# Two layers of attention, RWKV-7 and gated MLP on one core: a new order of emission in the mixings, and norm factors spread by VectorE

## The chip, the cores and the metric

The kernel runs on one core of one Trainium2 chip, in one launch. The metric is device time in microseconds (us), lower is better. Three runs of the kernel before took 2082.16, 2076.11 and 2067.94 us, median 2076.11 us.

## The reference, cut to what matters

There are 256 context tokens and 256 latent tokens of width 1024, and two layers. Each layer has a mixing part and a SwiGLU part. In the mixing part three branches read the same normalised input h: windowed attention, a bidirectional RWKV-7, and a spatial gating unit (SGU). They are merged by sigmoid gates and projected out. The RWKV branch sets the order of the work around the change:

```python
kk = heads((k * lp['k_k']).astype(f32))
kk = kk * lax.rsqrt(jnp.sum(kk * kk, -1, keepdims=True) + 1e-12)
...
S = S * w[..., None, :] + sa[..., :, None] * b[..., None, :] + v[..., :, None] * k[..., None, :]
...
mu = jnp.mean(y, -1, keepdims=True)
var = jnp.mean(jnp.square(y - mu), -1, keepdims=True)
y = ((y - mu) * lax.rsqrt(var + GN_EPS)).reshape(B, T, C) * lp['ln_w'] + lp['ln_b']
```

The state S passes through the context first and then through the latent tokens, in both directions. There are 8 heads of 64; the two `rsqrt` above give one factor for a head and a token.

## The kernel before, in words

Activations stand with channels on the 128 partitions and 512 tokens (context, then latent) in the free dimension. Dense products run as three fp32r products of split operands (high and low parts), so a weight tile of 128x1024 is loaded by SyncE's queue (`wtile`, L163), split by ScalarE (high part, L129) and VectorE (low part, L130), and used by 24 matmuls for one 128-row output (L92). Results go to two PSUM buffers with the tag `mm` that all dense products of the mixing share.

`phase_ab` (one call for each layer) holds the whole mixing up to the merge. It is written as Python generators, and each `yield` ends a stage:

- **K0 to K3** (`t_common`), one for a pair of heads: projections of k, r and v (stages 0 to 2; in layer 1 also the value residual in stage 2), norm of k (3 and 4), in-context rates (5), bonus (6). The norm is made by `rnorm` and `rnorm2`: squares are summed by TensorE (L423), the reciprocal root is computed by VectorE in some 12 small instructions (L136 to L142), GpSimd spreads it over 64 columns a head (the tile `rx`, L428), and TensorE transposes that (L436) for the multiplication.
- **P0 to P7** (`t_prep`), one for a unit, that is one pair of heads and one stream: unit 2h is pair h in the context, unit 2h+1 pair h in the latent tokens. Stage 0 makes the decay's matmuls (`pw`) and its tanh, stage 1 the cumulated decay (`pc`) and its exponentials, 2 the tile AR, 3 and 4 the tile BK with a scratch tile `gg` each, 5 to 8 four groups of score products (`psc`, L591, each taken from PSUM by VectorE into SC, L592), 9 to 11 transposes (`pvs`, `pbk`).
- **I0 to I7** (`t_inv`): a triangular inverse by VectorE, 31 steps of two dependent instructions (L645, L646), and small matmuls (`piy`, `pi`).
- **C0 to C7** (`t_chain`): four steps of the recurrence, each a few matmuls and short copies (`cw`, `cu`, `cn`, `py`); unit i waits for unit i-1.
- **Q0 to Q3** (`t_post`), a pair's end: group norm of y, also by `rnorm` and `rnorm2` (sums in `pm` and `gns`, scratch tiles `sqy` and `rx`), bonus, gate, and a store to DRAM by GpSimd's queue (L762).
- **G** (24 gate projections, tile `gps`, each stored by ScalarE's queue, L375), **A** (attention's q, k, v: matmuls `ptm`, transposes `pq`), **T** (attention: scores `sc`, transposes `pt`, output `po`), **S** (SGU), **X** (modulation vectors of layer 0, with weight loads on SyncE's queue).

The order is written out by hand. `slots` gives every stage a time from the numbers in `CB[layer]["SL"]`: pair h starts at `per`*h, K, P, C and Q are offsets, `P2` and `C2` shift the odd unit, the capital letters G, A, T, X, S start a series and the small letters are its steps. The stages are emitted by sorted time; `need` emits first what a stage depends on. The emitted program is then placed on the engines' queues, where a stage of a kind with a `PRI` of n is ranked as if it stood n instructions earlier; the dense matmuls of G and K keep their emitted order among themselves (`DENSE`). On chip each engine works through its queue in order.

Tiles with a tag share a few buffers: the tag `tmp` has 3 (`sgw`, `gg`, `sqk`, `sqy`, `rx`, `sm`, and in layer 1 `vf` and `sg`), the PSUM tags `rw` 1 (`pw`, `pc`, `psc`, `pvs`, `pbk`), `rc` 2 (`kns`, `knb`, `pa`, `pbn`, `pu`, `pm`, `gns`, `gnb`, `pg`, `pq`, `sc`, `pt`, `po`), `mm` 2. SC has 2 buffers, so unit i+2 can write its scores when unit i's chain has ended. The tile v has one buffer, so the next pair's v has to wait for the odd unit's `pvs`.

After `phase_ab` come `phase_m` (merge and output projection) and `phase_f` (SwiGLU), which the change does not touch.

Of the kernel before, what the change touches and what calls it, by code (L numbers as in the profile page):

```python
# [19 lines left out]
T = 256  # L20
# [7 lines left out]
DENSE = ("G", "K")  # L28
NX = 12
WR = 3  # L30
CB = [
    dict(SL={'per': 77.5, 'K': 10, 'P': 34.7, 'P2': 12, 'I': 108.0, 'C': 55.2, 'C2': 20, 'Q': 140, 'G': 120, 'g': 14, 'T': 120, 't': 4, 'A': 60, 'a': 5, 'S': 0, 's': 5.8, 'X': 60, 'x': 8},
         PRI={'C': 4000, 'I': 3000, 'P': 6000, 'K': 500, 'Q': 2000, 'T': 0, 'A': 0, 'S': 0, 'G': 0},
         PB={'rw': 1, 'rc': 2, 'ch': 1},
         GV=(1, 3),
         BF={'k': 2, 'v': 1, 'bv': 2, 'r': 1, 'kk': 2, 'th': 1, 'tmp': 3, 'ap': 2, 'aPT': 2, 'SC': 2, 'AR': 2, 'VS': 2, 'BKT': 2, 'BK': 1, 'ix': 1, 'gx': 1, 'gy': 1}),
    dict(SL={'per': 57.6, 'K': -18.7, 'P': 24.9, 'P2': 10.0, 'I': 95.9, 'C': 37.4, 'C2': 10.9, 'Q': 99.4, 'G': 62.8, 'g': 14.9, 'T': 73.7, 't': 6.1, 'A': 20, 'a': 4, 'S': -20, 's': 0.5, 'X': 32.2, 'x': 8},
         PRI={'C': 4000, 'I': 4000, 'P': 6000, 'K': 500, 'Q': 3000, 'T': 0, 'A': 0, 'S': 0, 'G': 0},
         PB={'rw': 1, 'rc': 2, 'ch': 1},
         GV=(1, 3),  # L40
         BF={'k': 2, 'v': 1, 'bv': 2, 'r': 1, 'kk': 2, 'th': 1, 'tmp': 3, 'ap': 2, 'aPT': 3, 'SC': 2, 'AR': 2, 'VS': 3, 'BKT': 2, 'BK': 1, 'ix': 2, 'gx': 1, 'gy': 1}),
]
DUR = dict(K=(5.5, 5.5, 5.5, 3, 1.5, 2, 5), P=(1.5, 2, 1, 3.5, 3.5, 1, 1, 1, 1, 1.5, 3, 1), I=(2.5,) * 9, C=(1.2,) * 12, Q=(2, 3, 1.5, 1), G=())


# [40 lines left out]
def trunk(ctx: ExitStack, tc: tile.TileContext, out, a):  # L86
# [11 lines left out]
    V = nc.vector  # L98
    S = nc.scalar
    G = nc.gpsimd  # L100
# [31 lines left out]
    def rsqrt(pool, out, x, scale, bias, tag):  # L132

        xs = pool.tile(list(out.shape), F32, tag=tag + "x", bufs=1, name="rsx")
        t = pool.tile(list(out.shape), F32, tag=tag + "t", bufs=1, name="rst")
        V.tensor_scalar(xs, x, scale * RS_A, bias * RS_A, op0=ALU.mult, op1=ALU.add)  # L136
        V.tensor_scalar(t.bitcast(I32), xs.bitcast(I32), 1, 0x7fffffff, op0=ALU.logical_shift_right, op1=ALU.bitwise_xor)
        V.tensor_scalar(out, t, RS_B, None, op0=ALU.mult)
        for _ in range(3):
            V.tensor_mul(t, out, out)  # L140
            V.scalar_tensor_tensor(t, t, -0.5 / RS_A, xs, op0=ALU.mult, op1=ALU.mult)
            V.scalar_tensor_tensor(out, t, 1.5, out, op0=ALU.add, op1=ALU.mult)  # L142
# [234 lines left out]
    def phase_ab(L, extra):  # L377

        l = L.l
        cb = CB[l]  # L380
        last = l == DEPTH - 1
# [3 lines left out]
        with tc.tile_pool(name="pb", bufs=1, reuse_waits="tile", side="right") as pb, tc.tile_pool(name="pe", bufs=1, reuse_waits="tile") as pe, tc.tile_pool(name="pbp", bufs=1, space=PSUM, reuse_waits="tile") as pbp:  # L385

            def rw(shape, name):
                return pbp.tile(shape, F32, tag="rw", bufs=cb["PB"]["rw"], name=name)

            def rc(shape, name):  # L390
                return pbp.tile(shape, F32, tag="rc", bufs=cb["PB"]["rc"], name=name) if "rc" in cb["PB"] else rw(shape, name)

            def tmp(name, n=512):
                return pe.tile([128, n], F32, tag="tmp", bufs=cb["BF"]["tmp"], name=name)

            def tmc(name, n=512):
                return pb.tile([128, n], F32, tag="tmc", bufs=cb["BF"]["tmc"], name=name) if "tmc" in cb["BF"] else tmp(name, n)

# [12 lines left out]
            def pj(f, s0, y):  # L411
                w = wtile(a["w_fm"][l, f])
                ps = pmm.tile([128, 512], F32, tag="mm", name="rps")
                n = 512 - 256 * s0
                proj(ps[:, :n], w, slice(256 * s0, 512), cl="K", l=l)
                conv(ps[:, :n], f, y, 2 - s0)

            def rnorm(sq, n, scale, bias, name):

                nt = n // 128  # L420
                pss = rc([128, 4, 2], name + "s")
                for j in range(nt):
                    mm(pss[:, j], sq[:, 128 * j:128 * j + 128], bones[:, 0:128:64], start=True, stop=True)  # L423
                rn = pb.tile([128, 4, 2], F32, tag="rn", bufs=2, name="rn")
                rsqrt(pb, rn[:, :nt], pss[:, :nt], scale, bias, "rr")
                rx = tmc("rx")
                rxv = rx[:, :n].rearrange("p (a h d) -> p a h d", h=2, d=64)
                G.tensor_tensor(rxv, rn[:, :nt].unsqueeze(3).broadcast_to([128, nt, 2, 64]),  # L428
                                ones[:, 0:64].unsqueeze(1).unsqueeze(1).broadcast_to([128, nt, 2, 64]), op=ALU.mult)
                return rx  # L430

# [16 lines left out]
            if last:  # L448

                vraw = tmc("vraw", KT * 32)  # L450
                nc.sync.dma_start(vraw, a["vrd"].rearrange("p k r -> p (k r)"))
                vhl = pe.tile([128, 512], F32R, tag="tmp", bufs=cb["BF"]["tmp"], name="vhl").rearrange("p (a b) -> p a b", a=2)
                vh, vl = vhl[:, 0], vhl[:, 1]
# [20 lines left out]
            def t_common(hp):  # L474

                h = H[hp]
                hc = slice(128 * hp, 128 * hp + 128)
                h.kT = kT = pe.tile([128, 512], F32, tag="k", bufs=cb["BF"]["k"], name="kT")
                pj(4 + hp, 0, kT)
                yield  # L480
                h.r = r = pe.tile([128, no], F32, tag="r", bufs=cb["BF"]["r"], name="r")
                pj(hp, so, r)
# [18 lines left out]
                sq = tmc("sqk")  # L501
                S.activation(sq, kT, AF.Square, scale=kkc)
                rx = rnorm(sq, 512, 1.0, 1e-12, "kn")
                yield
                rn = rnorm2(rx, 512, "kn")
# [173 lines left out]
            def t_chain(i):  # L679
# [8 lines left out]
                if emit:  # L688
                    py = pbp.tile([128, 8, 64], F32, tag="y", bufs=1, name="py")
                    mm(py.rearrange("p c j -> p (c j)"), zero, zero[:, 0:1].broadcast_to([1, 512]), start=True, stop=False)  # L690
                ch = lambda name: pbp.tile([128, 2, 64], F32, tag="ch", bufs=cb["PB"]["ch"], name=name)
                for c in range(4):
# [48 lines left out]
            def t_post(hp):  # L741

                need("C", 2 * hp + 1, 99)
                h = H[hp]
                y = h.y
                pm = rc([128, 512], "pm")
                mm(pm[:, :no], bones, y, start=True, stop=True)
                V.scalar_tensor_tensor(y, pm[:, :no], -1.0 / 64, y, op0=ALU.mult, op1=ALU.add)
                sq = tmc("sqy")
                S.activation(sq[:, :no], y, AF.Square)  # L750
                yield
                rx = rnorm(sq, no, 1.0 / 64, 64e-5, "gn")
                yield
                V.tensor_mul(y, y, rnorm2(rx, no, "gn"))
                V.tensor_scalar(y, y, pv[:, V_LW + hp:V_LW + hp + 1], pv[:, V_LB + hp:V_LB + hp + 1], op0=ALU.mult, op1=ALU.add)
                need("K", hp, 99)
                G.tensor_add(y, y, h.bv)
                yield
                pg = rc([128, 512], "pg")
                mm(pg[:, :no], L.gup[:, 128 * hp:128 * hp + 128], sxg, start=True, stop=True)  # L760
                V.tensor_mul(y, y, pg[:, :no])
                G.dma_start(orw_d[:, hp, 256 * so:512], y)  # L762
                yield
# [210 lines left out]
            def advance(kind, i):  # L974
# [3 lines left out]
                if done[key] == 99:  # L978
                    return
                with tc.high_priority(cb["PRI"].get(kind, 0)):  # L980
                    done[key] = 99 if next(live[key], live) is live else done[key] + 1
# [127 lines left out]
    with tc.tile_pool(name="px", bufs=1, side="right") as px, tc.tile_pool(name="pxp", bufs=1, space=PSUM) as pxp:  # L1109
        x = px.tile([128, KT, 512], F32, name="x0")  # L1110
# [17 lines left out]
    for l in range(DEPTH):  # L1128
# [8 lines left out]
        with tc.tile_pool(name="pw", bufs=1, reuse_waits="tile") as pw, tc.tile_pool(name="px", bufs=1, reuse_waits="tile", side="right") as px, tc.tile_pool(name="pxp", bufs=1, space=PSUM, reuse_waits="tile") as pxp:  # L1137
            x = px.tile([128, KT, 512], F32, name="x")
# [120 lines left out]
```

## Time and profile before

| what | value |
|---|---|
| median of three runs | 2076.11 us |
| the profiled execution's own time | 2055.66 us |
| its span, first to last instruction | 2053.9 us |
| TensorE (matmul) busy | 1913.0 us, 93% of the span |
| VectorE busy | 1355.0 us, 66% |
| ScalarE busy | 854.5 us, 42% |
| GpSimd busy | 237.7 us, 12% |
| mean granted TensorE clock | 0.943 |
| share of the last-ending chain: PE, DVE, DMA, ACT, issue, POOL | 74%, 12%, 4%, 4%, 4%, 1% |

The mixing of layer 0 lies between 48 us and 727 us of the span, that of layer 1 between 1245 us and 1775 us. PE is TensorE's matmuls, DVE VectorE, ACT ScalarE, POOL GpSimd. "Idle before" is the time in which an engine had nothing to run, and the name behind the arrow is what ended it.

### The profile page before, as it was taken

To read this page: it belongs to the slowest core of one execution; us is meant where nothing else is said; L and a number is where in the kernel's file an instruction comes from. 1 tells how busy PE (TensorE), PEld (TensorE's weight loads), DVE (VectorE), ACT (ScalarE), POOL (GpSimd) and SP (SyncE) were. 2 spreads that over 40 slices of the span, in tenths; PEclk is the share of its full clock that TensorE was granted. 3 is DMA by queue.
4 is the path that set the end of the run, shared out by engine and by line. 5 is a ranking of instruction groups with operands and counts; after the bars stand their busy time and mean duration, and the time that the engine had idled before them with its cause. 6 is when DMAs were issued, how large, how long until landed. Compare 5 with 4: busy or idle time off the path is not lost.

```text
span 2053.9 us, 35061 instructions
## 1 busy us (share of the span) xinstructions
PE 1913.0 (93%) x13162; PEld 1527.6 (74%) x13162; DVE 1355.0 (66%) x3657; ACT 854.5 (42%) x1848; POOL 237.7 (12%) x401
## 2 busy tenths in 40 slices
PE   4999989999999989899999997889998999698999
PEld 3877776666666768787887885777776777598999
DVE  4587776477585445688656545696786877476665
ACT  3442333444354433432232334444444555255443
POOL 3111201101001012100000002212020201120000
PEclk8997999989999999999999998988997999599999
DMA  8222213221211585166556422311220222374553
GB/s 286 78 67 79 63 47 114 83 90 53 63 39 55 202 269 163 62 188 212 176 175 212 145 79 76 100 66 32 93 69 14 74 75 88 122 230 146 185 183 105
DMA packets 97094, 239.16 MB, mean 116 GB/s; under 512 B 9594, under 2 KB 25082, under 8 KB 96796
## 3 DMA queue, kind: packets, MB, share of 16 engines
q1 hardware_dynamic: 88860, 223.82, 33.9%
q10 hardware_dynamic: 6912, 9.44, 1.3%
q0 software_dynamic: 1152, 3.67, 0.5%
q8 instruction: 103, 1.69, 0.3%
q14 instruction: 67, 0.55, 0.1%
HBM read 219.59 MB, written 17.30 MB: 115 GB/s over the span
## 4 chain that ended last, share of the span: by engine, by line
PE 74%; DVE 12%; DMA 4%; ACT 4%; issue 4%; POOL 1%; SPq 0%; ACTq 0%; POOLq 0%; DVEq 0%
PE fps L92 17%; PE gps L92 8%; PE rps L92 5%; PE psc L591 3%; PE yps L1094 3%; PE yps L1095 3%; PE yps L1096 3%; DVE wl L130 2%; PE sc L865 2%; DMA mr<-in_w_mod 2%; PE py L701 2%; PE po L893 2%; PE py L730 1%; PE cw L696 1%; PE ops L1026 1%
## 5 line engine op out<-in xcount | busy, mean ns | idle before, releaser
L129 ACT CAST wh<-wr 128x512 fp32r<-128x512 f32 (+1 forms) x560 | 341.7, 614 | 579.2 <-PE fps L92 196.8
L130 DVE TENSOR_TENSOR wl<-wr,wh 128x512 fp32r<-128x512 f32 (+1 forms) x560 | 389.6, 701 | 236.7 <-ACT wh L129 203.7
L92 PE MATMUL fps<-hh,wh 128*128 128x256 f32 (+1 forms) x720 | 241.3, 338 | 2.2 <-ACT hh L351 2.2
L92 PE MATMUL fps<-hh,wl 128*128 128x256 f32 (+1 forms) x720 | 241.6, 336 | 0.0
L92 PE MATMUL fps<-hl,wh 128*128 128x256 f32 (+1 forms) x720 | 240.9, 336 | 0.7 <-POOL hl L356 0.7
L92 PEld LDWEIGHTS fps<-hh,wh 128*128 128x128 f32 x720 | 138.3, 193 | 17.3 <-ACT hh L351 3.0
L92 PEld LDWEIGHTS fps<-hl,wh 128*128 128x128 f32 x720 | 138.3, 193 | 14.0 <-POOL hl L356 1.1
L92 PEld LDWEIGHTS fps<-hh,wl 128*128 128x128 f32 x720 | 138.7, 193 | 12.8
L92 PE MATMUL gps<-hh,wh 128*128 128x512 f32 (+1 forms) x384 | 142.1, 370 | 2.8 <-DVE itp L645 1.4
L92 PE MATMUL gps<-hl,wh 128*128 128x512 f32 (+1 forms) x384 | 140.1, 365 | 0.0
L92 PE MATMUL gps<-hh,wl 128*128 128x512 f32 (+1 forms) x384 | 139.0, 362 | 0.0
L1094 PE MATMUL yps<-fgh,wh 128*128 128x512 f32 (+1 forms) x352 | 118.7, 337 | 0.0
L1096 PE MATMUL yps<-fgh,wl 128*128 128x512 f32 (+1 forms) x352 | 118.3, 336 | 0.0
L1095 PE MATMUL yps<-fgl,wh 128*128 128x512 f32 (+1 forms) x352 | 118.3, 336 | 0.0
L271 DVE SCALAR_TENSOR_TENSOR macc<-mr,cr,macc 128x512 f32<-128x512 f32 x140 | 99.7, 747 | 22.0 <-DMA mr<-in_w_mod 21.4
L645 DVE TENSOR_TENSOR itp<-it,ix 128x60 f32<-128x60 f32 (+24 forms) x496 | 109.1, 222 | 7.1
L646 DVE TENSOR_TENSOR it<-it,itp 128x60 f32<-128x60 f32 (+24 forms) x496 | 108.1, 220 | 7.0
L92 PE MATMUL rps<-hh,wh 128*128 128x512 f32 (+1 forms) x224 | 91.5, 409 | 17.1 <-ACT hh L351 6.4
L92 PE MATMUL rps<-hl,wh 128*128 128x512 f32 (+1 forms) x224 | 91.2, 407 | 0.0
L92 PE MATMUL rps<-hh,wl 128*128 128x512 f32 (+1 forms) x224 | 90.3, 403 | 0.3 <-DVE wl L130 0.3
L92 PEld LDWEIGHTS gps<-hh,wh 128*128 128x128 f32 x384 | 74.6, 194 | 16.3 <-issue 2.6
L591 PE MATMUL psc<-AR,BK 64*128 64x128 f32 (+1 forms) x512 | 80.5, 302 | 6.6 <-DVE SC L592 1.4
(368 smaller groups left out, 4185.3 us busy)
## 6 DMA issues: line engine op xcount, KB each, us to landing
wr<-in_w SPq DMA_DIRECT2D x120, 512.0 KB, 3.5
wr<-in_w_fm SPq DMA_DIRECT2D x84, 512.0 KB, 3.5
mr<-in_w_mod SPq DMA_DIRECT2D x76, 512.0 KB, 4.4
wr<-in_w_o SPq DMA_DIRECT2D x24, 512.0 KB, 4.9
wr<-in_w_tm SPq DMA_DIRECT2D x20, 512.0 KB, 3.4
wr<-in_w_mod SPq DMA_DIRECT2D x20, 512.0 KB, 3.9
wr<-in_w_out SPq DMA_DIRECT2D x16, 512.0 KB, 4.0
gate_d<-gth ACTq DMA_DIRECT2D x24, 256.0 KB, 2.7
```

Source lines behind the costliest of these rows:

```text
L92: r = mm(*args, **kw)
L129: S.copy(hi, raw)
L130: (eng or V).tensor_sub(lo, raw, hi.bitcast(F32))
L271: V.scalar_tensor_tensor(acc[:, i], w, c[:, i:i + 1], acc[:, i], op0=ALU.mult, op1=ALU.add)
L591: mm(ps[:, c - c0, 0:64 * ns], BK[hs[x], c].rearrange("p a j -> p (a j)"), AR[hs[x], c, 0:ns].rearrange("p a j -> p (a j)"), start=True, s ...
L645: V.tensor_tensor(tv, Tm[:, t0:, s:s + 1].broadcast_to([128, n, s]), X[:, s, 0:s].unsqueeze(1).broadcast_to([128, n, s]), op=ALU.mult)
L646: V.tensor_tensor(Tm[:, t0:, 0:s], Tm[:, t0:, 0:s], tv, op=ALU.add)
L701: mm(py[hs[x], 4 * d + c], VS[hs[x], 4 * d + c, x], AR[hs[x], 4 * d + c, 1], start=False, stop=False)
L865: mm(sc, qT[p0:p0 + 64, pr, qs], kT[p0:p0 + 64, :kn], start=True, stop=qt < 2)
L1094: mm(ps[:, :n], wh, gh_[k][:, :n], start=k == 0, stop=False)
L1095: mm(ps[:, :n], wh, gl_[k][:, :n], start=False, stop=False)
L1096: mm(ps[:, :n], wl, gh_[k][:, :n], start=False, stop=k == nf - 1)
```

## The change: what it does

Numbers of `SL` change, so stages are emitted in another order; layer 1's K gets a `PRI` of 1500 for 500; and `rx` is written by VectorE, no longer by GpSimd. Buffers and `DUR` stay as they were.

```diff
-CB = [
-    dict(SL={'per': 77.5, 'K': 10, 'P': 34.7, 'P2': 12, 'I': 108.0, 'C': 55.2, 'C2': 20, 'Q': 140, 'G': 120, 'g': 14, 'T': 120, 't': 4, 'A': 60, 'a': 5, 'S': 0, 's': 5.8, 'X': 60, 'x': 8},
...
-    dict(SL={'per': 57.6, 'K': -18.7, 'P': 24.9, 'P2': 10.0, 'I': 95.9, 'C': 37.4, 'C2': 10.9, 'Q': 99.4, 'G': 62.8, 'g': 14.9, 'T': 73.7, 't': 6.1, 'A': 20, 'a': 4, 'S': -20, 's': 0.5, 'X': 32.2, 'x': 8},
-         PRI={'C': 4000, 'I': 4000, 'P': 6000, 'K': 500, 'Q': 3000, 'T': 0, 'A': 0, 'S': 0, 'G': 0},
...
+CB = [{'SL': {'per': 77.5, 'K': 10, 'P': 34.7, 'P2': 14.45, 'I': 108.0, 'C': 55.2, 'C2': 20, 'Q': 131.33, 'G': 120, 'g': 14.33, 'T': 120, 't': 4.17, 'A': 56.39, 'a': 5, 'S': 0, 's': 5.8, 'X': 60, 'x': 8},
...
+{'SL': {'per': 57.6, 'K': -18.7, 'P': 24.9, 'P2': 9.55, 'I': 95.9, 'C': 37.4, 'C2': 14.3, 'Q': 99.4, 'G': 62.8, 'g': 14.71, 'T': 73.7, 't': 6.1, 'A': 20, 'a': 4.04, 'S': -20, 's': 0.5, 'X': 33.89, 'x': 7.42},
+ 'PRI': {'C': 4000, 'I': 4000, 'P': 6000, 'K': 1500, 'Q': 3000, 'T': 0, 'A': 0, 'S': 0, 'G': 0},
...
@@ rnorm
                 rx = tmc("rx")
                 rxv = rx[:, :n].rearrange("p (a h d) -> p a h d", h=2, d=64)
-                G.tensor_tensor(rxv, rn[:, :nt].unsqueeze(3).broadcast_to([128, nt, 2, 64]),
+                V.tensor_tensor(rxv, rn[:, :nt].unsqueeze(3).broadcast_to([128, nt, 2, 64]),
                                 ones[:, 0:64].unsqueeze(1).unsqueeze(1).broadcast_to([128, nt, 2, 64]), op=ALU.mult)
```

What the new numbers do to the order in which each tag's buffers are asked for follows from `slots`, `need` and the stages alone (for P3.4 read stage 4 of P3):

- **Layer 1:** in `rw` the odd unit's `pc` moves ahead of the even unit's first `psc`, in all four pairs (before: pw odd, psc 1, pc odd, psc 2; after: pw odd, pc odd, psc 1, psc 2). The order in `tmp`, `rc`, `mm` and of the weight tiles is the same as before. The odd unit's last stages (P 10 to 12) and the even chain's last step (C 9 to 11) are now emitted ahead of the odd unit's inverse, not behind it, and with them the next pair's K.2, the pair's end Q.3 of the pair before and one gate.
- **Layer 0, `rw`:** `pw` of the odd unit moves from behind the even unit's first `psc` to behind the third, `pc` from behind the third to behind the even unit's `pvs`, in all four pairs.
- **Layer 0, `tmp`:** Q0's `sqy` and `rx` move ahead of the second `gg` of unit 3 (P3.4); the same for Q1 and unit 5, Q2 and unit 7.
- **Layer 0, `rc`:** Q0's `pm` moves from behind T's stage 4 to behind its stage 2, `gns` from behind stage 5 to behind stage 3, `gnb` and `pg` from behind stage 6 to around stage 4; the later pairs' ends move ahead by some stages of T too.
- **Layer 0, `mm` and weight tiles:** K1's k moves behind the four `ptm` of A's second column block; K2's v moves ahead of G's gate 4, K3's r ahead of gate 9, and one transpose of X (`mpt`) ahead of gate 2; one or two weight loads of X move by one place. Everything else keeps its place.

## Rows read from the trace of the kernel before

**Rows 1.** Busy time by stretch: us, each engine's busy us (instructions), PE clock, DMA share, GB/s.
```profile
48.00:300.00 252.00, 234.76 (x1642) 185.94 (x1642) 175.59 (x508) 96.30 (x212) 34.29 (x63) 0.92 0.23 71
300.00:727.00 427.00, 418.53 (x3037) 286.71 (x3036) 268.48 (x900) 191.00 (x467) 42.31 (x84) 0.98 0.27 89
1245.00:1742.00 497.00, 457.63 (x3528) 363.27 (x3530) 378.46 (x1253) 242.85 (x566) 86.61 (x152) 0.91 0.20 66
1742.00:1783.00 41.00, 28.78 (x250) 23.24 (x251) 14.45 (x48) 8.41 (x23) 4.12 (x9) 0.51 0.29 94
```

**Rows 2.** The tile gps on PE: count, duration ns min/median/max, first and last start us.
```profile
L92 PE MATMUL gps<-hh,wl x384: 274/389/583, 301.0 to 1738.3; 128*128 128x512 f32 x96, 128*128 128x256 f32 x96
```

**Rows 3.** Timeline of PE, end of layer 0's mixing: start us, us, engine line op.
```profile
695.43 0.49 PE L436 MATMUL gnb<-cst,rx 128*128 128x128 f32 x3
727.30 0.39 PE L92 MATMUL gps<-hh,wl 128*128 128x512 f32 x1
```

**Rows 4.** Timeline of ACT, Q0 and unit 3's second gg in layer 1.
```profile
1493.62 0.42 ACT L750 ACTIVATE sqy<-yo 128x256 f32<-128x256 f32 x1 [0.65 <-DVE yo L748]
1493.94 0.80 ACT L577 ACTIVATE gg<-th,al 128x512 f32<-128x512 f32 x1
```

**Rows 5.** The tile rx: its writer, and who waited for it (us, times).
```profile
L428 POOL TENSOR_TENSOR rx<-rn,ones x16: 613/1044/1519, 116.6 to 1772.7; 128x512 f32<-128x512 f32 x12, 128x256 f32<-128x256 f32 x4
  PE gnb L436: 4.3, 3
  PE knb L436: 3.6, 5
```

**Rows 6.** Timelines of POOL and DVE around rx in layer 1.
```profile
1523.73 1.52 POOL L428 TENSOR_TENSOR rx<-rn,ones 128x512 f32<-128x512 f32 x1 [3.70 <-DVE rn L142]
...
1524.27 1.06 DVE L645 TENSOR_TENSOR itp<-it,ix 128x63 f32<-128x63 f32 x1
1525.37 0.23 DVE L646 TENSOR_TENSOR it<-it,itp 128x63 f32<-128x63 f32 x1
...
1520.35 0.68 DVE L498 TENSOR_TENSOR v<-v,vf 128x512 f32<-128x512 f32 x1
```

**Rows 7.** Timelines of POOL and PE, units 4 and 5 in layer 1.
```profile
1543.78 0.62 POOL L550 TENSOR_SCALAR sgw__14748<-sgw__14748 128x512 f32<-128x512 f32 x1 [0.65 <-ACT sgw__14748 L549]
...
1545.60 0.85 PE L591 MATMUL psc<-AR,BK 64*128 64x64 f32 x6 [0.51 <-DVE BK L582]
...
1549.56 2.08 PE L556 MATMUL pc<-cst,sgw__14748 128*128 128x128 f32 x8
...
1553.23 0.77 PE L591 MATMUL psc<-AR,BK 64*128 64x64 f32 x5
```

**Rows 8.** Timeline of PE, unit 0's score products in layer 1 (third, fourth).
```profile
1346.05 1.10 PE L591 MATMUL psc<-AR,BK 64*128 64x64 f32 x8
...
1347.87 1.10 PE L591 MATMUL psc<-AR,BK 64*128 64x64 f32 x8
```

**Rows 9.** Timeline of PE, unit 0's score products in layer 0 (third, fourth).
```profile
139.84 1.16 PE L591 MATMUL psc<-AR,BK 64*128 64x128 f32 x8 [0.82 <-DVE SC L592]
...
146.29 1.16 PE L591 MATMUL psc<-AR,BK 64*128 64x128 f32 x8
```

**Rows 10.** Timelines of PE and DVE in layer 0: units 3 and 5, Q0.
```profile
296.86 1.13 PE L591 MATMUL psc<-AR,BK 64*128 64x128 f32 x8
...
364.26 0.28 PE L423 MATMUL gns<-cst,sqy 128*128 128x2 f32 x2
...
377.88 0.42 DVE L738 TENSOR_TENSOR yo<-yo,py 128x256 f32<-128x256 f32 x1 [0.49 <-ACT yo L737]
...
451.94 1.16 PE L591 MATMUL psc<-AR,BK 64*128 64x128 f32 x8
```

**Rows 11.** Timelines of PE and DVE: K3's v in layer 1.
```profile
1548.10 0.48 PE L92 MATMUL rps<-hh,wl 128*128 128x512 f32 x1
...
1614.35 0.74 DVE L409 SCALAR_TENSOR_TENSOR v<-rps,pv,v 128x510 f32<-128x510 f32 x1
```

More of the change, by code (lines that the diff above doesn't have):

```diff
@@ L30 @@
 WR = 3
-CB = [
-    dict(SL={'per': 77.5, 'K': 10, 'P': 34.7, 'P2': 12, 'I': 108.0, 'C': 55.2, 'C2': 20, 'Q': 140, 'G': 120, 'g': 14, 'T': 120, 't': 4, 'A': 60, 'a': 5, 'S': 0, 's': 5.8, 'X': 60, 'x': 8},
[L33 to L36, printed above, removed]
-    dict(SL={'per': 57.6, 'K': -18.7, 'P': 24.9, 'P2': 10.0, 'I': 95.9, 'C': 37.4, 'C2': 10.9, 'Q': 99.4, 'G': 62.8, 'g': 14.9, 'T': 73.7, 't': 6.1, 'A': 20, 'a': 4, 'S': -20, 's': 0.5, 'X': 32.2, 'x': 8},
-         PRI={'C': 4000, 'I': 4000, 'P': 6000, 'K': 500, 'Q': 3000, 'T': 0, 'A': 0, 'S': 0, 'G': 0},
[L39 to L42, printed above, removed]
+CB = [{'SL': {'per': 77.5, 'K': 10, 'P': 34.7, 'P2': 14.45, 'I': 108.0, 'C': 55.2, 'C2': 20, 'Q': 131.33, 'G': 120, 'g': 14.33, 'T': 120, 't': 4.17, 'A': 56.39, 'a': 5, 'S': 0, 's': 5.8, 'X': 60, 'x': 8}, 'PRI': {'C': 4000, 'I': 3000, 'P': 6000, 'K': 500, 'Q': 2000, 'T': 0, 'A': 0, 'S': 0, 'G': 0}, 'PB': {'rw': 1, 'rc': 2, 'ch': 1}, 'GV': (1, 3), 'BF': {'k': 2, 'v': 1, 'bv': 2, 'r': 1, 'kk': 2, 'th': 1, 'tmp': 3, 'ap': 2, 'aPT': 2, 'SC': 2, 'AR': 2, 'VS': 2, 'BKT': 2, 'BK': 1, 'ix': 1, 'gx': 1, 'gy': 1}}, {'SL': {'per': 57.6, 'K': -18.7, 'P': 24.9, 'P2': 9.55, 'I': 95.9, 'C': 37.4, 'C2': 14.3, 'Q': 99.4, 'G': 62.8, 'g': 14.71, 'T': 73.7, 't': 6.1, 'A': 20, 'a': 4.04, 'S': -20, 's': 0.5, 'X': 33.89, 'x': 7.42}, 'PRI': {'C': 4000, 'I': 4000, 'P': 6000, 'K': 1500, 'Q': 3000, 'T': 0, 'A': 0, 'S': 0, 'G': 0}, 'PB': {'rw': 1, 'rc': 2, 'ch': 1}, 'GV': (1, 3), 'BF': {'k': 2, 'v': 1, 'bv': 2, 'r': 1, 'kk': 2, 'th': 1, 'tmp': 3, 'ap': 2, 'aPT': 3, 'SC': 2, 'AR': 2, 'VS': 3, 'BKT': 2, 'BK': 1, 'ix': 2, 'gx': 1, 'gy': 1}}]
 DUR = dict(K=(5.5, 5.5, 5.5, 3, 1.5, 2, 5), P=(1.5, 2, 1, 3.5, 3.5, 1, 1, 1, 1, 1.5, 3, 1), I=(2.5,) * 9, C=(1.2,) * 12, Q=(2, 3, 1.5, 1), G=())
```

## The prediction, made before the run

> **What bounds the kernel now.** I read the page first: TensorE is busy for 93% of the span and makes 74% of the chain that ended last. So time can come only from two losses in the stages that the change touches: stretches in which TensorE waits, and stretches in which its clock is at the lower level. I then cut the span into stages [rows 1]. In layer 0 from 300 to 727 us TensorE is busy for 418.5 of 427 us at a clock of 0.98; what is saved on a wait of another engine there is worth next to nothing. From 48 to 300 us it idles 17.2 us at a clock of 0.92, and in layer 1 from 1245 to 1742 us 39.4 us at 0.91. The last 41 us of layer 1's mixing run at 0.51, the lower level (1.2 GHz), with 12.2 us idle: the gates are used up at 1738.3 us [rows 2] and only the last unit's chain and pair's end are left. Layer 0 ends the other way round: its last pair's end leaves TensorE at 695.9 us, and gates fill it densely until 727.7 us [rows 3]. Hence layer 0 has 31.4 us of slack in its recurrence at the end, and layer 1 has none.
>
> The timelines show one rule of this program that the argument needs: buffers of a tag are handed out in the order of emission. Unit 3's second `gg` in layer 1 ran at 1493.94 us, 0.32 us after `sqy` of Q0, which is emitted ahead of it, draws on the same three buffers and has nothing else to do with it, though P ranks 3000 above Q [rows 4]. So the orders listed with the change are what moves; a rank alone does not pass them.
>
> **The change part by part.** The sum is against the profiled execution's own time, 2055.7 us, which lies 20.4 us under the median of the three runs; I carry the difference over to the median, 2076.1 us.
>
> *Spreading by VectorE.* Sixteen GpSimd instructions go, 12 of 512 columns and 4 of 256, median 1.044 us [rows 5]. TensorE stood still for `rx` 8 times, 7.9 us in all [rows 5], part of it for the root that comes before `rx` and stays. A VectorE instruction with two SBUF inputs of 512 columns takes 0.68 us [rows 6]. Each wait shrinks by 1.04-0.68 = 0.36 us at least and, by the longest one, 1.52-0.68 = 0.84 us; the hand-over between engines that also goes is inside that spread. Eight waits give 2.9 to 6.7 us; I take -4. GpSimd's queue gets some 17 us emptier, which is worth nothing at 12% busy. VectorE gets 16 instructions, at most 16*0.68 = 10.9 us. But while `rx` ran on GpSimd, an instruction of the inverse took 1.06 us where its twin takes 0.23 [rows 6]: 0.83 us that goes with it, 13.3 us if it happened all 16 times. The net on VectorE lies between -2.4 and +10.9 us, half of it in layer 1, where VectorE is 76% busy and carries the inverses; I take +1, nearer the end that the row shows. The Trainium skill (SBUF — State Buffer, "Summary: rules for kernel authors") says that a VectorE instruction with two SBUF inputs and a GpSimd instruction that reads SBUF block each other, the second to issue waiting until the first ends. By it all 16 would block and this term would be -2 for +1; one row shows it and the sum does not rest on it.
>
> *Layer 1, `pc` of the odd unit ahead of the even unit's first score product.* In units 4 and 5 the odd tanh's scaling ended at 1544.40 us, the first `psc` ran at 1545.60, `pc` at 1549.56 and the second `psc` at 1553.23 [rows 7]. From `pc` to the next `psc` are 3.67 us, and a bare step from one `psc` to the next is 1.82 us [rows 8]. In the new order `pc` starts at 1544.40, the first `psc` at 1548.07, the second at 1549.89: 3.3 us earlier. The same arithmetic gives -0.7, -0.3 and +0.9 us for the other three pairs, where `psc` used a time in which `pc` was not ready. Together 3.2 us, on even units, which reach the end only through VectorE's time; bounds 0 and -6, I take -1.5.
>
> *Layer 0, `pw` and `pc` behind.* Third to fourth `psc` of unit 0 take 6.45 us with `pc` between [rows 9]; bare they take 1.82. So 4.6 us for each even unit's inverse. After 300 us it is hidden by full TensorE work; in the first pair TensorE lacks work, and I take -3 (bounds 0 and -4.6). The odd unit gets its decay later, behind the even unit's transposes, for which it waits anyway with BK's single buffer.
>
> *Layer 0, pairs' ends ahead of the odd unit's second `gg`.* This is the largest move. Unit 3's first score product stands at 296.86 us, and Q0's `gns` at 364.26 us, behind attention's third stage [rows 10]. Since `sqy` and `rx` of Q0 now come first in the scratch tiles, unit 3 cannot run its scores before about 364 us, unless attention itself comes earlier: 67.4 us later, its inverse and chain too. It ended at 378.3 us, and the next that needs it, unit 5's scores, started at 451.94 us [rows 10]: 73.6 us of slack, and 31.4 us at the layer's end. I cost it at nothing, hidden by unit 4's wait for K2 and by gates on TensorE; for units 5 and 7 the pair's end is ready about when they are. Q's store on GpSimd's queue moves with it, and nothing waits for it before the merge.
>
> *Rank of K in layer 1, places of A, G, T, X.* K3's v left TensorE at 1548.58 us and was taken out of PSUM at 1614.35 us, since its one buffer was held by unit 5's transposes [rows 11]. A higher rank does not bring that forward; weight tiles, `mm`, `rc` and `tmp` of layer 1 keep their order, loads on SyncE's queue too. I take 0, bounds -10 and +10: the 41 us at 0.51 at the end of layer 1 cost 20 us against the upper level [rows 1], and a stretch half as long more or fewer is as far as I let it go. Layer 0's one-place swaps of projections, gates and X's loads trade equal matmuls: 0. The even chain's last step ahead of the odd inverse: 0, under 2 us of VectorE either way.
>
> Sum: -4 +1 -1.5 -3 = -7.5 us: 2048 us for a profiled execution, **2068.6 us** for the median.
>
> **The rivals.** *Faster:* the odd units of layer 1 come earlier by more than the sum says, since K's small instructions now pass splits and attention on VectorE and ScalarE, and the last chain runs beside gates. For it speak 39.4 us idle and the clock of 0.91; against it the buffers' order. The last chain could move up to where the gates end, 36 us; half of that with the sum is -7.5-18: 2051 us. *Slower:* unit 3 of layer 0. If its late inverse (VectorE) and chain, now between 364 and 445 us, do not fit beside K2, unit 4 and attention but push them, the recurrence ends up to 67.4 us later, and all above 31.4 us comes out at the layer's end: +36 us, with the other terms 2105 us. It decides from a push of 31 us on; the two slacks together speak against it. *Inert:* the queues' order hardly changes where buffers decide, and only `rx` remains: 2073 us.
>
> **How the numbers follow.** About 1% (21 us) is what a measurement of this kernel tells from no change. Chances: forecast 0.35, inert 0.15, faster rival 0.30, slower rival 0.20. The forecast's own range is 2056 to 2080 us. The 8-in-10 range reaches to 2038 us, past the faster rival, and to 2100 us, which leaves out half of the slower one. Below 2055 us lie the faster rival and a little of the forecast, 0.34; above 2097 us most of the slower one, 0.18; between 0.48.
>
> **What would show it.** Right: no GpSimd `rx`, waits for `rx` on TensorE under 5 us; unit 3's scores in layer 0 at 350 us or later with layer 0's mixing still ending in a dense run of gates; the second `psc` of unit 4 in layer 1 closer behind the first. Wrong: layer 0's gates ending before the last pair's end; layer 1's mixing shorter by over 10 us with the last chain beside gates; inverses of odd units longer than before.

## The result and the profile after

The changed kernel takes **2055.3 us** (median of 10 runs, 2033.1 to 2084.8) beside 2073.6 us before (10 runs, 2063.4 to 2096.7): the ratio is 0.9886 with a 95% interval of 0.985 to 0.9923, 1.1% faster; the two medians alone give 0.9912. In a second series it was 2055.6 us (12 runs) beside 2073.5 us (35 runs), 0.9914 by the medians. The ratios with an interval leave out runs more than 1.5% above the fastest of their kernel, so in that series the ratio is 0.9952 (0.9919 to 0.9986) although the medians are 18 us apart as before.

The profiled execution of the changed kernel took 2060.9 us, 5 us *more* than that of before. The reason is in two rows of each page, the span with the granted clock and TensorE's busy time. The kernel before:

```profile
core 0: 2053.9 us, clock 0.943
```

```profile
PE 1913.0 (93%) x13162; PEld 1527.6 (74%) x13162; DVE 1355.0 (66%) x3657; ACT 854.5 (42%) x1848; POOL 237.7 (12%) x401
```

The changed kernel, first profile:

```profile
core 0: 2059.2 us, clock 0.932
```

```profile
PE 1935.4 (94%) x13162; PEld 1537.7 (75%) x13162; DVE 1354.9 (66%) x3673; ACT 854.3 (41%) x1848; POOL 221.5 (11%) x385
```

The changed kernel, profiled again in the second series:

```profile
core 0: 2038.3 us, clock 0.943
```

```profile
PE 1915.2 (94%) x13162; PEld 1523.0 (75%) x13162; DVE 1355.2 (66%) x3673; ACT 853.7 (42%) x1848; POOL 221.5 (11%) x385
```

TensorE idles 140.9 us before (2053.9 - 1913.0) and 123.8 and 123.1 us after: the change removes some 17.5 us of waiting. Its busy time for the same 13162 matmuls follows the clock. At the clock that the profile of before had, 0.943, the change is worth 15.6 us (2053.9 to 2038.3); at 0.932 all of it is eaten, and more.

So I compare all kernels below **at equal clock**. Every run lists its span and its mean granted clock. In the 174 runs of this study (one more, of the norm factors alone in the second series, at a clock of 0.821, is left out) the span is one offset for each kernel and series minus 1732 us for each 1.0 of clock, with 2.4 us left over (root mean square). The offsets are compared at 0.935; their 95% bounds are about 2 us. The changed kernel stands 15.9 and 15.4 us below the one before in its two series.

The stretches of [rows 1], first profile after (us, busy us (instructions) of TensorE, its weight loads, VectorE, ScalarE, GpSimd; TensorE's clock, DMA share, GB/s):

```profile
48.00:300.00 252.00, 238.68 (x1639) 182.90 (x1640) 169.47 (x502) 96.70 (x213) 30.49 (x61) 0.91 0.22 71
300.00:727.00 427.00, 422.84 (x3017) 287.64 (x3015) 272.15 (x915) 189.54 (x467) 38.21 (x78) 0.95 0.28 93
1245.00:1742.00 497.00, 463.20 (x3478) 367.19 (x3479) 373.82 (x1232) 236.95 (x553) 78.87 (x145) 0.88 0.19 63
1742.00:1783.00 41.00, 30.16 (x287) 24.48 (x285) 19.37 (x71) 12.85 (x32) 3.50 (x8) 0.65 0.28 97
```

Idle time falls by 3.9, 4.3 and 5.6 us in the first three, and the clock is lower in each of these three. (The windows are the same times, not quite the same work: 3478 matmuls of layer 1 lie in the third, where 3528 did.)

The rows that the prediction named for its steps, answering to [rows 5]: the writer of `rx` and what still waits for it on TensorE (a wait for `gnb`; in all it was 7.9 us before and is 2.9 us now).

```profile
L417 DVE TENSOR_TENSOR rx<-rn,ones x16: 424/685/1245, 116.9 to 1777.0; 128x512 f32<-128x512 f32 x12, 128x256 f32<-128x256 f32 x4
...
  PE gnb L425: 2.9, 1
```

Layer 0, answering to [rows 10] and [rows 3]: Q0's `gns`, unit 3's and unit 5's first score products, the last pair's end, and the last gate.

```profile
320.56 0.95 PE L412 MATMUL gns<-cst,sqy 128*128 128x2 f32 x8
...
337.88 1.43 PE L580 MATMUL psc<-AR,BK 64*128 64x128 f32 x5
...
470.56 1.13 PE L580 MATMUL psc<-AR,BK 64*128 64x128 f32 x8 [0.33 <-DVE itp L634]
...
681.52 0.63 PE L425 MATMUL gnb<-cst,rx 128*128 128x128 f32 x4
...
733.38 0.39 PE L81 MATMUL gps<-hh,wl 128*128 128x512 f32 x1
```

Unit 3 moved back from 296.9 to 337.9 us, and the layer still ends in 51 us of dense gates. Layer 1, answering to [rows 7]: unit 5's decay product now stands ahead of unit 4's score products, and these follow one another 1.8 us apart.

```profile
1556.44 1.16 PE L545 MATMUL pc<-cst,sgw__14748 128*128 128x128 f32 x8
...
1559.08 0.77 PE L580 MATMUL psc<-AR,BK 64*128 64x64 f32 x5
...
1560.87 1.10 PE L580 MATMUL psc<-AR,BK 64*128 64x64 f32 x8
```

### The profile page after: what moved, and what is told of

Its sections match the earlier page's. It is cut to its first block, busy times and chain, and to the rows that moved or that the text cites. A ratio compares the mean times of both kernels' runs of the same rounds, so it can differ in the third digit from the quotient of the medians.

```text
span 2059.2 us, 35050 instructions
## 1 busy us (share of the span) xinstructions
PE 1935.4 (94%) x13162; PEld 1537.7 (75%) x13162; DVE 1354.9 (66%) x3673; ACT 854.3 (41%) x1848; POOL 221.5 (11%) x385
## 5 line engine op out<-in xcount | busy, mean ns | idle before, releaser
L81 PEld LDWEIGHTS fps<-hl,wh 128*128 128x128 f32 x720 | 138.2, 193 | 14.1 <-POOL hl L345 1.2
L81 PE MATMUL rps<-hh,wh 128*128 128x512 f32 (+1 forms) x224 | 95.7, 427 | 17.3 <-ACT hh L340 6.4
```

Of the source, the lines that this page charges most:

```text
L81: r = mm(*args, **kw)
```

## The experiments

Three series of four, each series on one chip with runs of the kernel before. The table is the summary; "rx" stands for the norm factors on VectorE, "L0" and "L1" for the new numbers of a layer. The ratios of the first four are those of the medians, without an interval.

| kernel | runs | median us | ratio to before (95%) | mean clock | at equal clock, us | TensorE idle in the profile, us |
|---|---|---|---|---|---|---|
| before, three series | 63 | 2076.7 | 1 | 0.933 | 0 | 140.9 |
| rx | 6 | 2044.5 | 0.981 | 0.946 | -9.1 | 136.6 |
| L0 | 6 | 2074.1 | 0.9955 | 0.928 | -4.8 | 135.1 |
| L1 | 6 | 2061.2 | 0.9893 | 0.937 | -7.6 | 133.9 |
| L0 and L1 | 6 | 2072.7 | 0.9948 | 0.929 | -10.0 | 130.0 |
| rx, again | 12 | 2046.9 | 0.9917 (0.9884-0.995) | 0.945 | -8.0 | 136.5 |
| whole change, again | 12 | 2055.6 | 0.9952 (0.9919-0.9986) | 0.936 | -15.4 | 123.1 |
| rx and L1 | 12 | 2041.4 | 0.9885 (0.9844-0.9926) | 0.945 | -11.1 | 134.7 |
| rx and L0 | 12 | 2055.8 | 0.9921 (0.9877-0.9964) | 0.938 | -14.1 | 126.2 |
| rx with a shadow on GpSimd | 6 | 2045.5 | 0.9893 (0.9841-0.9945) | 0.945 | -7.4 | 139.7 |
| rx, L1, of L0 only P2 | 12 | 2051.6 | 0.9903 (0.9858-0.9949) | 0.942 | -6.0 | 128.4 |
| rx, L1, of L0 only Q, A | 6 | 2046.7 | 0.9887 (0.9832-0.9942) | 0.940 | -16.6 | 131.0 |
| rx, L1, of L0 only g, t | 6 | 2048.5 | 0.9884 (0.9829-0.994) | 0.940 | -11.2 | 133.0 |

Idle time in one profile and the offset at equal clock are two separate readings of the waiting. As differences to the kernel before they agree within 2.5 us for five of the twelve, within 4 us for seven and within 7 us for all.

**First series: each part alone**, on another chip than the two later series. Theory A: TensorE waits less, each part in its own place. Theory B: all of the gain is the norm factors' move. Theory C: the same work, another draw of the clock.

The norm factors alone (L428):

```diff
-                G.tensor_tensor(rxv, rn[:, :nt].unsqueeze(3)...
+                V.tensor_tensor(rxv, rn[:, :nt].unsqueeze(3)...
```

> Before with only the norm factors spread by VectorE; numbers of both orders as before. Theory A (the gain is waiting time of TensorE, some of it behind rx): ratio to before 0.996 to 0.998, 4 to 8 us, TensorE's wait for rx at most half of the 7.9 us. Theory B (the whole gain is the removed GpSimd instruction, with the VectorE instructions that it held up): 0.987 to 0.991, some 23 us. Theory C (the gain is a different draw of stretches at the lower clock): 0.99 to 1.01 with the whole difference in the granted clock, and the same time as before at the same clock.

Layer 0's numbers alone:

```diff
-'P2': 12,    'Q': 140,    'g': 14,    't': 4,    'A': 60
+'P2': 14.45, 'Q': 131.33, 'g': 14.33, 't': 4.17, 'A': 56.39
```

> Before with only the new numbers of layer 0; rx on GpSimd, layer 1 as before. Theory A: ratio 0.996 to 0.998, 5 to 8 us, from idle time of TensorE in layer 0's mixing (30.9 us before, 23.7 us in the changed kernel). Theory B: 1.000. My slower rival (unit 3 held behind pair 0's end): above 1.000. Unit 3's first score product moves from 297 us to 335 us or later in either case.

Layer 1's numbers alone (with the rank of K):

```diff
-'P2': 10.0, 'C2': 10.9, 'g': 14.9,  'a': 4,    'X': 32.2,  'x': 8;    PRI 'K': 500
+'P2': 9.55, 'C2': 14.3, 'g': 14.71, 'a': 4.04, 'X': 33.89, 'x': 7.42; PRI 'K': 1500
```

> Before with only the new numbers of layer 1, the rank of K among them (which by itself leaves every engine's queue as it was); rx on GpSimd, layer 0 as before. Theory A: ratio 0.994 to 0.998, 4 to 12 us, from idle time of TensorE in layer 1's mixing (52.7 us before, 42.6 us in the changed kernel, rx's part included). Theory B: 1.000.

Both layers' numbers, the norm factors still on GpSimd:

> Both layers' new numbers, rx left on GpSimd. If the parts add up, its ratio is the product of the two single layers' ratios, and with rx's ratio it gives 0.9886. Theory A: 0.990 to 0.995. Theory B: 1.000. If rx and the orders depend on each other (the queues are placed anew each time), the product misses 0.9886 by more than 0.004.

The norm factors alone gave 0.981, more than the whole change, and the ratios do not multiply up: 0.981 * 0.9948 is 0.976, and the medians of the whole change give 0.991. B fell with it (layer 1 alone is 7.6 us down at equal clock), and A's ratios were missed in three of four. TensorE's wait for `rx`, which A put at half of 7.9 us at most, was 4.7 us:

```profile
  PE gnb L436: 3.1, 2
...
  PE knb L436: 1.6, 1
```

At equal clock the parts come near to sums: -9.1, -4.8 and -7.6, the two layers together -10.0 (for -12.4), the whole change -15.9 (for -21.5), and clocks that differ between kernels. That is A for the waiting, and a new question for the clock: luck of a series (C), or theory D, a property of the order of work.

**Second series: the same again, and pairs.** The edits are those above, combined.

> Same kernel as the first run of the norm factors on VectorE alone; there its median stood at 0.981 of the kernel before, with a median granted clock of 0.946 against 0.929, and a line through the runs (about -1800 us per 1.0 of granted clock) put it only 8 us below the kernel before at the same clock. Theory C (the higher clock was a draw of that series): 0.994 to 0.998 here, clock within 0.005 of the kernel before. Theory D (this kernel is granted a higher clock as a property of its order of work): again 0.978 to 0.985 and a clock 0.012 to 0.02 above the kernel before. Both: 5 to 11 us less at equal clock.

> The whole change, in one series with its parts. Theory A (less waiting of TensorE, the parts add up at equal clock): 13 to 19 us below the kernel before at equal granted clock, so ratio 0.987 to 0.995, and 5 to 11 us below the norm factors on VectorE alone at equal clock. Theory B (the norm factors' move is the whole gain): no more than 2 us from the norm factors alone at equal clock.

> Layer 1's numbers and the norm factors on VectorE, layer 0's numbers as before. Theory A: the sum of the two parts alone, 8 + 7.5 = about 15 us below the kernel before at equal granted clock (11 to 18). Theory B: 8 us. If layer 0's new order costs clock (theory D), the granted clock here is above that of the whole change by 0.008 or more.

> Layer 0's numbers and the norm factors on VectorE, layer 1's numbers as before. Theory A: 8 + 5 = about 13 us below the kernel before at equal granted clock (9 to 16). Theory B: 8 us. If layer 0's new order costs clock (theory D), the granted clock here is no higher than that of the whole change, and below that of the norm factors alone by 0.008 or more.

The norm factors alone came out at 2046.9 us and a clock of 0.945 again, where 35 runs of the kernel before had 0.933: C falls, D stands, although the ratio with its interval, 0.9917, lies between what C and D expected. D's sign for norm factors and layer 1 came (0.009 above the clock of the whole change); those for norm factors and layer 0 were just missed (0.007 below the norm factors alone, 0.008 expected; 0.002 above the whole change, "no higher" expected). At equal clock A holds for layer 0, which adds 5 to 6 us to the norm factors (-14.1 against -8.0 to -9.1) and 4 to 5 us to both others (-15.4 to -15.9 against -11.1). It fails for the pair of norm factors and layer 1: -11.1, the lower edge of what it expected, where the parts alone sum to -16. The two overlap, as below.

For the clock the four pairs with and without layer 0's numbers say the same: 0.933 to 0.928, 0.937 to 0.929, 0.945 to 0.938 and 0.945 to 0.935, on average 0.0075 lower, or 13 us given back. The four pairs with and without the norm factors' move: 0.933 to 0.945, 0.937 to 0.945, 0.928 to 0.938, 0.929 to 0.935, on average 0.009 higher, 16 us gained. Layer 1's numbers change it by less than 0.004 in every pair. (The kernel before itself had 0.929, 0.933 and 0.935 in the three series, so a single pair across series is loose. Fitted to the 117 runs of the first two series, with a term for each series, the move is worth +0.011 of clock, layer 0's numbers -0.007 and layer 1's +0.001, each 0.003 either way at 95%.)

**A version that beats both kernels** follows: norm factors and layer 1's numbers, layer 0 as it was. It took 2041.4 us, and in the same series its mean is 11.1 us (7.4 us either way, 95%) below the whole change, though it waits more.

Where layer 0's numbers lose the clock is seen in the changed kernel's first profile, cut at the falls of the clock (columns as above):

```profile
180.00:214.00 34.00, 31.92 (x311) 25.74 (x308) 26.21 (x109) 10.24 (x24) 5.10 (x12) 1.00 0.15 48
215.00:252.00 37.00, 36.93 (x229) 22.10 (x228) 14.54 (x45) 8.21 (x20) 4.92 (x9) 0.50 0.09 28
253.00:323.00 70.00, 67.78 (x499) 49.01 (x499) 50.51 (x178) 30.37 (x75) 4.89 (x11) 1.00 0.31 99
324.00:364.00 40.00, 40.00 (x192) 25.77 (x192) 17.25 (x42) 7.51 (x24) 3.86 (x6) 0.50 0.12 40
365.00:420.00 55.00, 54.56 (x448) 35.72 (x449) 30.77 (x123) 21.18 (x56) 5.18 (x13) 1.00 0.21 64
```

For 37 and for 40 us TensorE is busy without a pause and runs at the lower level all the same (0.50, 1.2 GHz). The kernel with norm factors and layer 1 alone, over the same part:

```profile
180.00:260.00 80.00, 75.81 (x727) 55.96 (x727) 60.03 (x212) 28.74 (x64) 13.77 (x26) 1.00 0.16 49
260.00:340.00 80.00, 75.82 (x613) 56.51 (x615) 60.52 (x217) 28.41 (x73) 6.32 (x15) 0.96 0.27 88
340.00:420.00 80.00, 77.86 (x586) 52.05 (x588) 45.88 (x144) 36.51 (x95) 7.87 (x16) 1.00 0.24 77
```

It waits more here (10.5 us of 240 against 4.8 of 236) and hardly loses clock. What TensorE did before each fall, changed kernel, first profile (start, us, engine, line; in brackets the idle time before and what ended it):

```profile
213.74 0.55 PE L832 MATMUL pq<-cst,qx 128*128 128x128 f32 x3 [2.08 <-DVE qx L827]
214.12 1.38 PE L115 MATMUL piy<-it,cst 128*128 128x256 f32 x4
215.43 1.73 PE L652 MATMUL piy<-it,SC 32*32 32x32 f32 x32
...
320.56 0.95 PE L412 MATMUL gns<-cst,sqy 128*128 128x2 f32 x8
...
322.51 1.09 PE L661 MATMUL pi<-TT,it 32*32 32x32 f32 x32
323.53 0.45 PE L685 MATMUL cw<-VS,SC 128*64 128x64 f32 x4
323.91 0.79 PE L81 MATMUL gps<-hh,wl 128*128 128x512 f32 x1
```

The first fall comes right behind a wait of 2.08 us for the attention's queries. The second comes behind no wait, but behind small products of the inverse and the pair's end, which stand together there. In the changed kernel's second profile the first stretch is the same (213 to 249 us at 0.50), and the second is all but gone:

```profile
213.00:249.00 36.00, 35.93 (x220) 21.84 (x219) 14.21 (x42) 7.27 (x18) 4.75 (x9) 0.50 0.07 22
250.00:321.00 71.00, 68.95 (x523) 50.08 (x520) 51.42 (x182) 30.57 (x75) 4.87 (x11) 1.00 0.32 103
325.00:420.00 95.00, 94.56 (x753) 62.63 (x752) 59.70 (x187) 38.20 (x99) 10.80 (x21) 1.00 0.24 77
```

The other profiles tell what is order and what is draw. All five with the whole of layer 0's numbers (the changed kernel twice, L0 alone, L0 and L1, rx and L0) have the 2.08 us wait, a fall of the clock within 1 us of its end, and a second fall at 316 to 334 us with TensorE busy without a pause in the 8 us before. The six with layer 0 as it was have neither. What differs between executions is how long the clock stays at 0.50: 14 to 38 us after the first fall, 3 to 44 us after the second. From 200 to 400 us the mean granted clock is 0.79 to 0.92 in the five and 0.93 to 0.98 in the six.

**Third series: why the norm factors, and which part of layer 0.** The shadow is this, on the kernel with the norm factors alone:

```diff
                 V.tensor_tensor(rxv, rn[:, :nt].unsqueeze(3)...
+                rd = pb.tile([128, 2, 64], F32, tag="rd", bufs=1, name="rd")
+                for z in range(nt):
+                    G.tensor_tensor(rd, rn[:, z]..., ones[:, 0:64]..., op=ALU.mult)
```

> Norm factors on VectorE, and behind each of them GpSimd makes the same product again into a tile that nobody reads (in four pieces of 128x128). Theory L (the gain is that the path to TensorE's transposes is shorter): as the norm factors on VectorE alone, 6 to 10 us below the kernel before at equal granted clock, clock about 0.945. Theory S (the gain is that GpSimd no longer lengthens VectorE's instructions beside it): 0 to 4 us below at equal clock, and VectorE's instructions under the product are lengthened again, by some 5 to 8 us over all sixteen.

It cost little or nothing: -7.4 beside -8.0 and -9.1 us, a difference of 1.0 us with 2.3 us either way, clock 0.945. GpSimd and VectorE did meet. Timelines of the shadow kernel, VectorE and then GpSimd, in layer 1:

```profile
1514.48 0.92 DVE L428 TENSOR_TENSOR rx<-rn,ones 128x512 f32<-128x512 f32 x1
1515.33 0.41 DVE L645 TENSOR_TENSOR itp<-it,ix 128x60 f32<-128x60 f32 x1
```

```profile
1514.46 2.62 POOL L429 TENSOR_TENSOR rd<-rn,ones 128x128 f32<-128x128 f32 x4 [3.79 <-DVE rn L142]
```

The same two instructions with no shadow (second run of the norm factors alone):

```profile
1510.62 0.68 DVE L428 TENSOR_TENSOR rx<-rn,ones 128x512 f32<-128x512 f32 x1
1511.22 0.21 DVE L645 TENSOR_TENSOR itp<-it,ix 128x60 f32<-128x60 f32 x1
```

Over all, 21 VectorE instructions under the shadow lost 4.3 us against the median of their kind; before, ten instructions under GpSimd's `rx` lost 6.7 us. That brings back two thirds of the lengthening. If S were the whole gain, two thirds of it, over 5 us, should have been lost: so S falls as the whole of it, though a smaller part is not excluded. (The shadow is in four pieces, so single delays are shorter than before.) An emptier GpSimd queue is not the gain either: with the shadow GpSimd is busy for 254.3 us, before for 237.7. L, the shorter path to TensorE's transposes, is left by elimination and not shown by itself: TensorE's waits for `rx` shrink by only 3.2 us, and the new place of `rx` in VectorE's queue was not tried apart.

The parts of layer 0, each on top of norm factors and layer 1:

```diff
-'P2': 12
+'P2': 14.45
...
-'Q': 140,    'A': 60
+'Q': 131.33, 'A': 56.39
...
-'g': 14,    't': 4
+'g': 14.33, 't': 4.17
```

> Norm factors and layer 1's numbers, and of layer 0's only the second stream's preparation (P2). The kernel with none of layer 0's stood 11 us below the kernel before at equal granted clock with a median clock of 0.946, the whole change 15 us below with 0.934. Theory A: the 4 us come from whichever part takes away the 3.9 us wait for the modulation's weights at 260 us; without it -9 to -13 us at equal clock. Theory D: this part does not bring the half-clock stretches at 210 to 250 and 320 to 365 us, clock 0.942 to 0.948; if it does, 0.930 to 0.938.

> Norm factors and layer 1's numbers, and of layer 0's only Q (a pair's end) and A (the attention's steps) emitted earlier. Theory D as I take it: the half-clock stretch at 210 to 250 us follows a 2.08 us wait of the transposes pq for qx, an operation of the attention's preparation, so this part carries the lower clock: 0.930 to 0.938, and -11 to -16 us at equal clock; ratio 0.990 to 0.997. If the clock stays at 0.942 to 0.948 it is another part.

> Norm factors and layer 1's numbers, and of layer 0's only the gates' and the projections' steps (g, t). Theory D as I take it: clock 0.942 to 0.948, no half-clock stretch of over 20 us at 210 to 250 us; -9 to -14 us at equal clock; ratio 0.985 to 0.990. If it brings the stretches, 0.930 to 0.938.

The pair's end and the attention (Q, A) bring the gain of layer 0 at equal clock: -16.6 against -11.1 us without them. Gates and projections do nothing (-11.2). The second stream's preparation came out worse by 5 us at equal clock, although its profile idles least of the three; these two readings contradict each other, and I leave it open. Nor do the parts add up: +5.1, -5.5 and -0.1 us come to -0.5, where all of them together give -4.3 to -4.8. One wait is a candidate for the place of the gain, that of TensorE for the modulation's weights (total us, times, longest us). Kernel before:

```profile
PE mps L251 <- DMA wr<-in_w_mod: 4.4, 2, 3.9
```

The changed kernel:

```profile
PE mps L240 <- DMA wr<-in_w_mod: 1.0, 2, 0.5
```

With g and t only it is as before, with Q and A only it is 1.9 us. With P2 only it is gone, and yet nothing was gained. So this wait explains idle time in the profiles, and that it carries the gain at equal clock is not shown.

```profile
PE mps L251 <- DMA wr<-in_w_mod: 4.0, 1, 4.0
```

```profile
PE mps L251 <- DMA wr<-in_w_mod: 1.9, 1, 1.9
```

The clocks, 0.942, 0.940 and 0.940, lie between those with and without the whole of layer 0's numbers (0.942 or more was expected of the first and the last). I had expected Q and A to carry the loss at 0.930 to 0.938: missed in the mean, though their profile has a stretch at 0.50 of its own, behind a wait of 2.13 us (the wait in the timeline, then the stretch):

```profile
220.06 1.13 PE L126 MATMUL piy<-it,cst 128*128 128x256 f32 x4 [2.13 <-DVE it L646]
```

```profile
222.00:272.00 50.00, 49.91 (x293) 31.54 (x293) 19.70 (x68) 8.73 (x22) 4.01 (x9) 0.50 0.13 42
```

From 200 to 400 us, where the whole of layer 0's numbers lose the clock, the profiles have 0.95 with P2, 0.87 with Q and A and 0.98 with g and t. So one profile each points at Q and A; with 6 to 12 runs, and series that differ by as much, the mean clocks do not confirm it.

**Layer 1's overlap with the norm factors.** Its mixing ends with a tail: after the last gate only the last unit's chain and pair's end are left. Last gate product and last `gnb` (the end of each row's range), norm factors alone:

```profile
L92 PE MATMUL gps<-hh,wl x384: 276/389/583, 298.3 to 1717.0; 128*128 128x512 f32 x96, 128*128 128x256 f32 x96
L436 PE MATMUL gnb<-cst,rx x24: 272/286/474, 366.9 to 1753.0; 128*128 128x128 f32 x24
```

Whole change, second profile:

```profile
L92 PE MATMUL gps<-hh,wl x384: 274/389/793, 301.0 to 1731.2; 128*128 128x512 f32 x96, 128*128 128x256 f32 x96
L436 PE MATMUL gnb<-cst,rx x24: 270/273/474, 327.8 to 1758.2; 128*128 128x128 f32 x24
```

This tail is 36.2 us before, 35.3 to 36.1 with the norm factors and layer 1 as before, some 32 with layer 1's numbers and GpSimd's `rx`, and 27.0 to 27.6 in all six profiles that have both. Its length is not time saved: of the 9 us that both take from it, 2.3 are waiting (TensorE idles 9.3 us in it before, 6.9 to 7.1 after), and the rest is work that now runs ahead of the last gate (242 matmuls in it before, 186 after). What is saved shows in the idle time. In layer 1, from its first `ups` product to the last `gnb`, TensorE idles 39.1 us before, 35.1 to 35.6 with the norm factors, 33.0 to 33.1 with layer 1's numbers, and 32.6 to 34.6 in the six with both: 3.5 to 4.0 and 6.0 to 6.1 us less alone, 4.5 to 6.5 together. Where layer 1's numbers are in, the norm factors save hardly any more waiting there.

## Why the prediction was right or wrong

The time, 2055.3 us, lies in the range (2038 to 2100) and just below the forecast's own, 2056 to 2080; the forecast, 2068.6, saw 7.5 us where 18 came. Split by cause, 15.5 us come at equal clock and 3.6 us (0.0021 of mean clock) through the clock, 19 in all. That the clock adds so little is luck as far as the forecast goes: the norm factors' move gains 16 us by it and layer 0's numbers give 13 back, and the sum had neither.

*Spreading by VectorE: the parts right, the whole too small.* I took -4 for TensorE's waits; with the norm factors alone 4.7 of 7.9 us are left, -3.2, and 2.9 with the whole change, -5.0. I took +1 for VectorE; its busy time rose by 2.3 and 2.6 us in the two profiles (1355.0 to 1357.3 and 1357.6). But alone the move is worth 8 to 9 us at equal clock, where idle time accounts for 4.4, and then 0.009 of clock, 16 us more. The first surplus is not located. For the second, no term of the sum stood for the clock outside the end of layer 1; that is what failed most.

The timeline of before bears out the rule that I quoted from the Trainium skill (SBUF — State Buffer, "Summary: rules for kernel authors"), but not my reading of it, that all 16 would block. Of the sixteen, ten met a VectorE instruction that then ended after GpSimd's; six met none at all or only instructions that read PSUM, and those ran at their usual length. The lost 6.7 us lie between the one row's 0.83 and the 13.3 us of all 16, and the shadow, which brought 4.3 us of such delays back, cost 1.0 us with 2.3 us either way.

*Layer 1: mis-sized.* The step "reach the end only through VectorE's time" gave -1.5 us. Layer 1's numbers alone give -7.6 at equal clock, 2 to 3 on top of the norm factors. The score products moved together as worked out, and TensorE idles 6 us less in layer 1, so the term is too small by some 6 us alone and by 1 on top of the norm factors. Which hand-over brings it no run isolates. The faster rival named the place: the last chain did move up beside the gates, by 9 of the 36 us, but most of that is work moved and not time saved.

*Layer 0: right size, other place.* -3 forecast, -4.8 alone, 4 to 6 on top of the others. I had put it down to the decay products in the first pair. In idle time the largest piece is another, the modulation's weights, for which TensorE waited 3.94 us at 260 us and now 0.5; I had not costed that row. That it is also the gain at equal clock is not shown, since with P2 alone the wait is gone and nothing is gained. The large move was judged rightly: unit 3's scores came 41 us later (at 337.9 us, where I had named 350 or later: Q0's `gns`, for which it waits, came at 320.6 instead of 364.3), and the layer's end still lies in dense gates. But the same numbers lower the clock, 13 us by the four pairs; nothing in the sum could show that.

*Rank of K, and the rest.* With the rank back at 500 the changed kernel's instructions stand in the same order on every engine; it does nothing, as argued. (The bound of 10 us was drawn from 20 us that the stretch at 0.51 should cost; a faster clock shortens only its 28.8 us of work, so it is some 14.)

*The rivals.* The slower one did not happen: gates end layer 0 at 733.4 us, 51 us after the last pair's end. Of the signs of being wrong one came in part: in the first profile after, the inverses of odd units take 35.5 us on average in layer 1, for 33.6 before (unit 3's 38.5 for 29.6), while in layer 0 they take 30.4 for 35.0. Inert (2073 us) falls with the 15.5 us. The faster one came true in its place, in part. "Below 2055 us" had a chance of 0.34 and the stretch above it 0.48: the terms that I had came to twice their sum, the clock added the rest, and the result, 2055.3 us, stands at that very bound (0.9912 by the medians, 0.9886 by the ratio with its interval).

What stays open: why the norm factors' move raises the granted clock, where half of its gain at equal clock lies, which hand-over gives layer 1's gain, and why the second stream's preparation alone loses at equal clock.

## What to carry to other kernels

Where a kernel is bound by TensorE, list the granted clock of every run and compare versions at equal clock first: parts whose ratios made no sense (0.981 alone, 0.991 with everything) became differences that TensorE's idle time bears out in the main. Then look at what each part does to the clock by itself, for an order that waits less can also run more of its work at the lower level: leaving layer 0's new numbers out was 11 us faster than the whole change. Two changes that each remove waiting in the same layer need not add: the norm factors and layer 1's numbers, 8 to 9 and 7.6 us alone, gave 11.1 together. And a shorter tail is not yet time saved: look at how much of it was waiting.

## What the runs showed of the hardware

- TensorE ran at 1.2 GHz (0.50) for 37 to 50 us on end while busy for 99.8 to 100% of it (36.93 of 37, 40.00 of 40, 49.91 of 50 us); the falls came behind a wait of about 2.1 us, or with TensorE busy without a pause in the 8 us before (small products among its work). The place of a fall was the same in five profiles with the same order of layer 0, and its length, 3 to 44 us, was not.
- One kernel's executions differ by their clock and little else: 0.919 to 0.953 for the kernel before, 1732 us per 1.0, 2.4 us left over.
- A GpSimd product of 1.04 us holds up even a VectorE instruction of 128x8 (0.17 us, then 1.05), while VectorE instructions that read PSUM under such a product kept their length (`VS` 0.29 us at 371.3 us, `SC` 0.69 us at 1711.3 us, both the median of their kind). Timelines of VectorE and GpSimd, kernel before:

```profile
247.33 0.17 DVE L136 TENSOR_SCALAR rsx<-ssq 128x8 f32<-128x8 f32 x1
247.53 1.05 DVE L137 TENSOR_SCALAR rst<-rsx 128x8 int32<-128x8 int32 x1
```

```profile
247.51 1.04 POOL L428 TENSOR_TENSOR rx<-rn,ones 128x512 f32<-128x512 f32 x1 [6.87 <-DVE rsx L136]
```
